# Broadcasts of norm roots as transposes, state-space products by row halves, and sample's score pairs, in one layer of a hybrid encoder

## The chip, the cores and the metric

The kernel runs on one core of one Trainium2 chip. The metric is the time of one execution on the device in microseconds (us). The core has a matrix engine (TensorE, PE in the profile, whose weight loads are listed apart as PEld), VectorE (DVE), ScalarE (ACT), GpSimd (POOL) and SyncE (SP). SyncE issues the DMAs here, in order. Each engine works through its own queue in order and waits on semaphores for the others.

## The reference

One inference step of one layer (depth 1, width 1024, float32) for 2048 prompt frames and 32 sample frames that continue a stream of 2048 earlier frames:

```python
h = x + RMSNorm(Mixer(RMSNorm(x)))
y = h + RMSNorm(ConvFFN(RMSNorm(h)))
```

The mixer makes one input projection and runs two groups of 8 heads of 64 beside each other. Group A is stick-breaking attention: with scores z, the weight of key k is sigmoid(z_k) times the product of sigmoid(-z_j) over all later keys j up to the query, strictly causal. Group B is a state-space scan (Mamba-2) in 2 groups of 4 heads with state 64, behind a causal convolution of width 4. Both outputs are RMS-normalised and projected. The ConvFFN is a gated MLP with hidden width 2816 and a causal convolution of width 3 on the gate.

Three things in it matter here. Every RMSNorm needs, for each frame, the root 1 / sqrt(mean of squares + eps). In each chunk of the scan, `cb = C B^T` and `C h` are needed for each of the two groups of heads, where h is the state. The 32 sample frames attend to 2048 cached keys of 8 heads.

## The kernel before

**Tiling.** Features lie on the partitions and frames along the free axis. The 2080 frames are cut into four blocks of 512, 512, 512 and 544 (`SBS`; the last holds the 32 sample frames). Matrix products are exact in float32 by splitting both operands into a high and a low part; `dense` (line 180) multiplies the three products that matter. The attention's products (lines 910, 951) work on such parts too. Small products are plain float32 matmuls.

**Stages.** `phase_in` goes over the four blocks: norm, projection, convolution, the state-space chunks of 128 frames (16 of the prompt and one of sample, 32 frames wide), keys and queries, gate. Then `Attention.heads(0, ...)` runs the first block's attention in 32 slots (8 heads x 4 query blocks); the last block's gate is woven into it as a filler, and every third slot takes one step of `sample`. From then on `heads(s)` for the next block is woven with `Tail.stream` of the block before (output projection, residual, norms, the gated MLP). The last block's tail runs alone (`Tail.alone`, from about 2380 us).

**Order.** The program is written in this order, but the order of each engine's queue is made by the planner of the compiler from a simulated timeline (`schedule_with_timeline_sim=True`). `pin`, `mark` and `behind` add dependencies that keep some fillers behind a given matmul.

**Norm roots** (`rstd_steps`, lines 214 to 273). Line 222 sums the squares over the partitions: each block of 128 frames gives one column of up to 128 rows. GpSimd raises to the power -1/2 (line 245) into `v`. Line 257 then spreads each column over all 128 partitions: a matmul with the column, read as 128 equal columns, as the stationary operand and the identity as the moving one:

```python
mm = nc.tensor.matmul(
    ps[:, c0 : c0 + q], v[:, b : b + 1].to_broadcast([P, P]), self.ident[:, :q], start=True, stop=True
)
```

It is called for the norm of each input block (4 or 5 columns), for the gate's norm of the last block (5), and for each half of each block in `norm_in`, `residual`, `root` and `finish` (2 columns, or 3 with a narrow one of 16 rows in the last block). The tiles are named `st`, `o` and `u` in the profile, the column `rn_v` or `rn_w`.

**State-space products** (lines 536 to 546). For each chunk, group g uses partitions 64 g to 64 g + 63: one product of line 540 (`cb`) and two of line 542 (`C h`), first all three of group 0, then all three of group 1. Each group writes a PSUM bank of its own. VectorE reads both behind them.

**Sample's scores** (`sample`, lines 794 to 831). Five pieces of keys (32 new ones, then four of 512) by two groups of four heads make ten steps. A step takes two loads `sk` of 256 KB (tile of 128 x 512, two buffers, lines 805 to 808), and each of them feeds one matmul of line 809 that fills one half of the partitions of the score tile `z`. Then follow the sigmoids, the scan (line 761), transposes (line 820) and the product with the values (line 825). The values' loads `sv` (line 800) have four buffers.

Of the kernel before, what the change touches and what calls it, by code (L numbers as in the profile page):

```python
# [8 lines left out]
F32 = mybir.dt.float32  # L9
# [23 lines left out]
P = 128  # L33
# [6 lines left out]
DH = 64  # L40
# [30 lines left out]
class Kernel:  # L71
# [139 lines left out]
    def rstd_steps(self, pool, psp, pt, sq, n, width, tag="rstd", out=None, rcol=None, of=None, stay=False, pin=False):  # L211

        nc = self.nc
        nb = (n + P - 1) // P
        nf, e = divmod(n, P)
        ps = psp.tile([P, 512], F32, name=pt)
        for b in range(nb):
            q = min(P, n - b * P)  # L220
            for i, t in enumerate(sq):
                mm = nc.tensor.matmul(  # L222
                    ps[:q, b : b + 1], t[:, b * P : b * P + q], self.ones[:, 0:1],
                    start=i == 0, stop=i == len(sq) - 1,
                )
                if pin and b + i == 0:
                    self.pin(mm)
        if pin:
            self.mark(mm)
        v = pool.tile([P, 8], F32, name="rn_v")  # L230
        if e:
            nc.vector.memset(v[:], 1.0)
        for rows, cols in ((slice(0, P), slice(0, nf)),) + (((slice(0, e), slice(nf, nb)),) if e else ()):
            if of is None:
                nc.vector.tensor_scalar(
                    v[rows, cols], ps[rows, cols], 1.0 / width, EPS, op0=ALU.mult, op1=ALU.add
                )
            else:
                nc.vector.scalar_tensor_tensor(
                    v[rows, cols], ps[rows, cols], 1.0 / width, of[rows, cols], op0=ALU.mult, op1=ALU.add  # L240
                )
        w = v
        if rcol is not None:
            w = pool.tile([P, 8], F32, name="rn_w")
        nc.gpsimd.tensor_tensor(w[:, :nb], v[:, :nb], self.mhalf[:, :nb], op=ALU.pow)
        if rcol is not None:
            nc.gpsimd.tensor_scalar(rcol[:, :nb], v[:, :nb], EPS, 0.0, op0=ALU.mult, op1=ALU.add)
        v = w
        yield
        ps = psp.tile([P, 512], F32, name=pt)  # L250
        r = ps if stay else pool.tile([P, 544], F32, name=tag) if out is None else out
        for b in range(nb):
            q = min(P, n - b * P)
            if b == 4:
                nc.scalar.copy(r[:, :512], ps[:])
            c0 = b % 4 * P
            mm = nc.tensor.matmul(
                ps[:, c0 : c0 + q], v[:, b : b + 1].to_broadcast([P, P]), self.ident[:, :q], start=True, stop=True
            )
            if pin and b == 0:  # L260
                self.pin(mm)
        if pin:
            self.mark(mm)
        if nb == 5:
            nc.scalar.copy(r[:, 512:n], ps[:, : n - 512])
        elif not stay:
            nc.scalar.copy(r[:, :n], ps[:, :n])
        self.rcol = v
        yield r


def phase_in(kn, ctx):
    nc, tc, a, o = kn.nc, kn.tc, kn.a, kn.o
# [102 lines left out]
    for s, (t0, nt) in enumerate(SBS):  # L376
# [25 lines left out]
        for c, then in zip(order, (*order[1:], None)):  # L402
# [5 lines left out]
            for c0, c1 in tiles_of(nt):  # L408
                ps = psd.tile([P, 512], F32, name="o")
# [34 lines left out]
        for b in range(nb):  # L444
            q = min(P, nt - b * P)
# [3 lines left out]
            for h in range(2):  # L449
                for k in range(KC):  # L450
                    for i, (l, rr) in enumerate(((xhi, wv[0]), (xlo, wv[0]), (xhi, wv[1]))):
                        nc.tensor.matmul(  # L452
                            vp[h][:q, :260], l[k][:, b * P : b * P + q], rr[:, k, h * 260 : h * 260 + 260],
                            start=i == 0 and k == 0, stop=i == 2 and k == KC - 1,
                        )
            v = sd.tile([P, 520], F32, name="v")
# [40 lines left out]
        ps = psm.tile([P, 512], F32, name="st")  # L497
# [10 lines left out]
        ps = psm.tile([P, 512], F32, name="st")  # L508
# [6 lines left out]
        for b in range(nb):  # L515
            q = min(P, nt - b * P)
# [18 lines left out]
            nc.scalar.activation(eA[:, :, :q], eA[:, :, :q], AF.Exp)  # L535
            h_in = hS if b == 4 else hT[state["h"]]
            cy = psy.tile([P, 2, 512], F32, name="y")
            for g in range(2):
                rows = slice(g * 64, g * 64 + 64)
                nc.tensor.matmul(cy[:q, g, :q], bc[rows, 0, sl], bc[rows, 1, sl], start=True, stop=True)  # L540
                for i in range(2):
                    nc.tensor.matmul(
                        cy[:, g, P + i * q : P + i * q + q],
                        h_in[rows, 2 * i : 2 * i + 2, :].rearrange("p h d -> p (h d)"), bc[rows, 1, sl],
                        start=True, stop=True,
                    )
# [14 lines left out]
            ps = psm.tile([P, 512], F32, name="st")  # L561
# [11 lines left out]
            ps = psm.tile([P, 512], F32, name="st")  # L573
# [41 lines left out]
        for name, dst in (("wk", kn.kS), ("wq", kn.qS)):  # L615
            for c in range(4):
# [4 lines left out]
                for c0, c1 in tiles_of(nt):  # L621
                    ps = psd.tile([P, 512], F32, name="o")
                    kn.dense(ps, w, xs, c0, c1)
                    n = c1 - c0
# [83 lines left out]
class Attention:  # L708
# [60 lines left out]
    def sample(self, ctx, pu):  # L769
# [22 lines left out]
        for kc in (4, 3, 2, 1, 0):  # L792
# [7 lines left out]
                    nc.sync.dma_start(v[i][:], a["cvv"][:, 4 * kc + i, :])  # L800
            for g in range(2):
                z = self.pz.tile([P, 512], F32, name="z")
                for i in range(2):
                    c = 2 * g + i
                    k = kp.tile([P, 512], F32, name="sk", bufs=2)
                    nc.sync.dma_start(
                        k[:, :n], kn.kF[:, c, :] if kc == 4 else a["ck"][c][:, 512 * kc : 512 * kc + 512]
                    )
                    nc.tensor.matmul(
                        z[DH * i : DH * i + DH, :n], qp[:, c, :], k[:, :n], start=True, stop=kc < 4  # L810
                    )
                if kc == 4:
                    nc.tensor.matmul(z[:, :n], kn.identb[:], mk[:], start=False, stop=True)
                w, end = self.weights_of(z[:, :n], n, prev[g], own[g])
# [855 lines left out]
```

## Time and profile before

| what | us |
|---|---|
| median of 3 runs | 2902.88 |
| lowest, highest | 2899.2, 2905.06 |
| the profiled execution | 2897.34 |
| its span, from the first to the last instruction | 2895.5 |

The profile shows that one execution. TensorE's mean granted clock in it is 0.985 of full speed. The page's first part gives, for each engine, busy time, share of the span and number of instructions. The page's chain follows the work that ended last back to the start, and gives its shares by engine. A row of a group reads: line, engine, operation, output <- inputs, rows*columns of the array that are used and shapes, count | busy us, mean ns of one | idle us of the engine just before them and what ended that. A row of the timeline reads: start, length, engine, line, operation, tiles, count, and in brackets an idle time before it. In a view by stretches each row has a stretch's length, the busy time of the five engines with their counts, the granted clock, the share of the DMA engines and GB/s. Bars of matmuls that follow each other overlap.

### The profile page before, as it was taken

The page shows a single profiled execution, that of the slowest core. Times are in us where ns is not written, and L with a number is a line of the kernel's source. Part 1 is how long each engine was busy: PE and PEld are TensorE (multiplying, and loading weights), DVE is VectorE, ACT ScalarE, POOL GpSimd, SP SyncE. Part 2 cuts the span into 40 slices and gives each one's busy share as a digit, 9 for nine tenths or more (in the row PEclk, how much of TensorE's full clock was granted, in tenths as well). Part 3 has the DMA queues.
Part 4 walks back from the last instruction along what each step waited for, and adds up shares of the span by engine and source line. Part 5 has one row for each costly group of instructions (what it writes and reads, how often), then busy time and mean ns, then how long its engine had stood idle before and what let it go on. Part 6 is the DMA issues. An engine that isn't in the chain of part 4 may idle for free.

```text
span 2895.5 us, 46167 instructions
## 1 busy us (share of the span) xinstructions
PE 2798.5 (97%) x16771; PEld 2416.4 (83%) x16771; DVE 1651.0 (57%) x2628; ACT 1217.8 (42%) x2568; POOL 1134.5 (39%) x1065
## 2 busy tenths in 40 slices
PE   7999999988999999999999999989999999999998
PEld 6878789976978888887888888978888889999997
DVE  7594747367564554557555555785666653623333
ACT  4343434246555454455433334654444443321111
POOL 3534242224566666556322223453223323511113
PEclk9999999999999999999999999999999999999999
DMA  8889695878767787875755556666555555755566
GB/s 291 269 303 304 240 305 206 244 227 263 233 232 265 273 273 253 274 257 192 227 169 182 183 179 227 207 202 196 172 168 171 167 176 184 249 178 178 170 177 204
DMA packets 348644, 642.04 MB, mean 222 GB/s; under 512 B 73498, under 2 KB 192930, under 8 KB 338690
## 3 DMA queue, kind: packets, MB, share of 16 engines
q1 hardware_dynamic: 348418, 639.09, 67.9%
q8 instruction: 134, 2.20, 0.3%
q14 instruction: 92, 0.75, 0.1%
HBM read 482.40 MB, written 156.57 MB: 221 GB/s over the span
## 4 chain that ended last, share of the span: by engine, by line
PE 77%; DVE 11%; DMA 6%; issue 3%; ACT 2%; POOL 1%; SPq 1%; DVEq 0%; ACTq 0%; POOLq 0%
PE o L180 39%; PE u L180 12%; PE t L180 11%; PE z L910 4%; PE pa L951 4%; PE pt L929 4%; DVE xc L425 2%; PE o L452 1%; DMA acB<-acD 1%; DVE prow L761 1%; DVE xlo L1099 1%; DVE f L1427 1%; DMA vS<-vs 1%; DMA o_kT<-kf 1%; PE u L222 1%
## 5 line engine op out<-in xcount | busy, mean ns | idle before, releaser
L180 PE MATMUL o<-xhi,w 128*128 128x512 f32 (+2 forms) x3968 | 1041.2, 344 | 17.9 <-ACT xhi L355 7.7
L180 PEld LDWEIGHTS o<-xhi,w 128*128 128x128 f32 x3968 | 694.4, 191 | 111.1 <-ACT xhi L355 7.7
L180 PE MATMUL o<-xlo,w 128*128 128x512 f32 (+2 forms) x1984 | 679.7, 343 | 1.5 <-DVE xlo L356 1.1
L766 POOL TENSOR_TENSOR beta<-beta,prow 128x512 f32<-128x512 f32 (+3 forms) x256 | 255.9, 1000 | 511.1 <-DVE prow L761 427.9
L180 PEld LDWEIGHTS o<-xlo,w 128*128 128x128 f32 x1984 | 377.6, 190 | 44.4 <-DVE xlo L356 1.6
L180 PE MATMUL u<-xhi,w 128*128 128x512 f32 x1056 | 351.3, 398 | 0.0
L180 PE MATMUL o<-ah,w 128*128 128x512 f32 x992 | 342.7, 402 | 3.4 <-DVE f L1395 3.3
L161 POOL TENSOR_TENSOR w<-wraw,w 128x512 fp32r<-128x512 f32 (+3 forms) x178 | 243.1, 1368 | 155.2 <-ACT w L160 127.8
L1347 POOL TENSOR_TENSOR y<-y,gb 128x512 f32<-128x512 f32 (+1 forms) x88 | 116.0, 1318 | 457.7 <-ACT gb L1346 457.4
L934 DVE TENSOR_TENSOR wt<-pt,wt 128x512 fp32r<-128x512 f32 (+2 forms) x320 | 191.6, 601 | 155.0 <-ACT wt L933 153.0
L761 DVE TENSOR_TENSOR_SCAN prow<-gam,prow,z 128x513 f32<-128x513 f32 x192 | 245.0, 1277 | 58.4 <-ACT beta L759 58.1
L933 ACT CAST wt<-pt 128x512 fp32r<-128x512 f32 (+2 forms) x320 | 167.3, 525 | 237.8 <-PE pt L929 235.9
L180 PEld LDWEIGHTS u<-xhi,w 128*128 128x128 f32 x1056 | 198.6, 188 | 46.2
L180 PEld LDWEIGHTS o<-ah,w 128*128 128x128 f32 x992 | 187.1, 189 | 45.8 <-DVE f L1395 4.4
L180 PE MATMUL u<-xlo,w 128*128 128x512 f32 x528 | 209.1, 396 | 0.0
L758 ACT ACTIVATE gam<-z 128x512 f32<-128x512 f32 (+2 forms) x320 | 173.0, 541 | 66.0 <-PE z L910 40.0
L180 PE MATMUL o<-al,w 128*128 128x512 f32 x496 | 196.7, 396 | 0.0
L180 PE MATMUL t<-xhi,w 128*128 128x272 f32 x960 | 189.4, 293 | 3.3 <-DMA w<-wS_outw 2.1
L929 PE MATMUL pt<-ident,beta 128*128 128x128 f32 x1088 | 182.8, 277 | 4.7 <-DVE wt L934 4.6
L1339 DVE SCALAR_TENSOR_TENSOR y<-gb,cv,y 128x512 f32<-128x512 f32 (+1 forms) x176 | 143.2, 813 | 69.1 <-ACT y L1337 66.0
L951 PE MATMUL pa<-wt,v 128*64 128x256 f32 (+3 forms) x1152 | 173.2, 281 | 7.7 <-DVE wt L934 5.5
L160 ACT CAST w<-wraw 128x512 fp32r<-128x512 f32 (+3 forms) x178 | 113.0, 635 | 158.5 <-PE o L180 93.1
(288 smaller groups left out, 4907.6 us busy)
## 6 DMA issues: line engine op xcount, KB each, us to landing
w<-wS_up SPq DMA_DIRECT2D x264, 512.0 KB, 3.5
w<-wS_dn SPq DMA_DIRECT2D x144, 384.0 KB, 3.5
w<-wS_outw SPq DMA_DIRECT2D x94, 512.0 KB, 6.2
wS_up<-w SPq DMA_DIRECT2D x88, 512.0 KB, 3.6
wraw<-wup SPq DMA_DIRECT2D x88, 256.0 KB, 4.2
k<-kS SPq DMA_DIRECT2D x80, 256.0 KB, 3.8
v<-vS SPq DMA_DIRECT2D x80, 256.0 KB, 3.7
w<-wS_bx SPq DMA_DIRECT2D x18, 1024.0 KB, 5.3
```

What stands on the lines that cost most here:

```text
L161: nc.gpsimd.tensor_tensor(lo, raw[:, :m, :], hi.bitcast(F32), op=ALU.subtract)
L180: mm = nc.tensor.matmul(ps[:, : c1 - c0], l, r, start=first and i == 0 and k == 0, stop=last and i == 2 and k == len(w) - 1, **({"skip_gro ...
L758: nc.scalar.activation(g[:, c0:512], z, AF.Sigmoid, scale=-0.125)
L761: nc.vector.tensor_tensor_scan(back(pr), back(g), z[:, 0:1].to_broadcast([P, n + 1]), self.kn.ones[:, 0:1] if prev is None else prev, op0= ...
L766: eng.tensor_tensor(b[:, :n], b[:, :n], pr[:, c0 + 1 : 513], op=ALU.mult)
L910: mm = nc.tensor.matmul(z[:, :n], q[:, P * b : P * b + P], k[:, :n], start=e == 0, stop=e == 1 and kc < s)
L929: mm = nc.tensor.transpose(t[:, P * j : P * j + P], w[:, P * j : P * j + P], kn.ident[:])
L933: nc.scalar.copy(hi, t)
L934: kn.exit = nc.vector.tensor_tensor(lo, t, hi.bitcast(F32), op=ALU.subtract)
L951: nc.tensor.matmul(av[:m, 2 * P * p + c0 : 2 * P * p + 2 * P], v[:, j, :m], wt[:, rest, j, c0:], start=kc == s and p + j + rest == 0, stop ...
L1339: nc.vector.scalar_tensor_tensor(y[:, :W], gb[:, i : i + W], kn.col(wc + i), y[:, :W], op0=ALU.mult, op1=ALU.add)
L1347: nc.gpsimd.tensor_tensor(y[:, :W], y[:, :W], t, op=ALU.mult)
```

## The change

```diff
             c0 = b % 4 * P
-            mm = nc.tensor.matmul(
-                ps[:, c0 : c0 + q], v[:, b : b + 1].to_broadcast([P, P]), self.ident[:, :q], start=True, stop=True
-            )
+            mm = nc.tensor.transpose(ps[:, c0 : c0 + q], v[:q, b : b + 1].to_broadcast([q, P]), self.ident[:q, :q])
...
-            for g in range(2):
-                rows = slice(g * 64, g * 64 + 64)
+            half = [slice(g * 64, g * 64 + 64) for g in range(2)]
+            for g, rows in enumerate(half):
                 nc.tensor.matmul(cy[:q, g, :q], bc[rows, 0, sl], bc[rows, 1, sl], start=True, stop=True)
-                for i in range(2):
+            for i in range(2):
+                for g, rows in enumerate(half):
                     nc.tensor.matmul(
                         cy[:, g, P + i * q : P + i * q + q],
...
             for g in range(2):
                 z = self.pz.tile([P, 512], F32, name="z")
-                for i in range(2):
-                    c = 2 * g + i
-                    k = kp.tile([P, 512], F32, name="sk", bufs=2)
-                    nc.sync.dma_start(
-                        k[:, :n], kn.kF[:, c, :] if kc == 4 else a["ck"][c][:, 512 * kc : 512 * kc + 512]
-                    )
-                    nc.tensor.matmul(
-                        z[DH * i : DH * i + DH, :n], qp[:, c, :], k[:, :n], start=True, stop=kc < 4
-                    )
+                k = kp.tile([P, 2, 512], F32, name="sk", bufs=2)
+                src = kn.kF[:, 2 * g : 2 * g + 2, :]
+                if kc < 4:
+                    src = a["ck"][2 * g : 2 * g + 2, :, 512 * kc : 512 * kc + 512].rearrange("c p n -> p c n")
+                nc.sync.dma_start(k[:, :, :n], src)
+                for c0 in range(0, n, 256):
+                    c1 = min(n, c0 + 256)
+                    for i in range(2):
+                        nc.tensor.matmul(
+                            z[DH * i : DH * i + DH, c0:c1], qp[:, 2 * g + i, :], k[:, i, c0:c1],
+                            start=True, stop=kc < 4,
+                        )
```

The first edit spreads a column by a transpose: the column's q rows, read as 128 equal columns, are transposed against the q x q identity, so that 128 partitions get q equal rows. The second one issues the products of the two groups in turn: both `cb`, then both first products with the state, then both second ones. The third one loads the keys of both halves of a score tile by one DMA of 512 KB into one tile (two buffers of 128 x 2 x 512, twice the memory), and multiplies them in pieces of 256 keys, the halves in turn.

## The prediction

> **What bounds the kernel now.** I read the page first, then the busy time by stage, then TensorE's groups by line, and last the timeline at the three places that the change touches.
>
> ```profile
> span 2895.5 us, 46167 instructions
> PE 2798.5 (97%) x16771; PEld 2416.4 (83%) x16771; DVE 1651.0 (57%) x2628; ACT 1217.8 (42%) x2568; POOL 1134.5 (39%) x1065
> ...
> PE 77%; DVE 11%; DMA 6%; issue 3%; ACT 2%; POOL 1%; SPq 1%; DVEq 0%; ACTq 0%; POOLq 0%
> ```
>
> TensorE is busy for 97% of the span, and 77% of the chain that ended last is its own work; VectorE and the DMAs hold most of the rest. So a matmul that goes is worth time in most places, but not in all. The stages say where, in this view by stretches (length, TensorE busy, weight load, VectorE, ScalarE, GpSimd, clock, DMA):
>
> ```profile
> 0.00:600.00 600.00, 569.86 (x3489) 483.14 (x3489) 382.72 (x708) 236.51 (x397) 223.63 (x165) 0.99 0.80 266
> 600.00:726.00 126.00, 109.26 (x767) 85.09 (x764) 84.72 (x141) 74.05 (x189) 49.38 (x65) 0.91 0.82 259
> 726.00:2380.00 1654.00, 1625.86 (x8724) 1362.96 (x8723) 981.41 (x1347) 790.31 (x1727) 725.07 (x701) 0.99 0.65 211
> 2380.00:2896.00 516.00, 493.54 (x3803) 485.20 (x3802) 202.19 (x434) 116.95 (x256) 136.44 (x135) 0.98 0.62 195
> ```
>
> 0 to 600 us is the input phase with the state-space chunks: 30 us idle. 600 to 726 is sample's attention woven into the first attention block: TensorE idles 16.7 of 126 us, and the granted clock is lowest, 0.91. The two stretches behind hold nearly all the norm roots and leave TensorE idle 28 and 22 us. "Busy" needs care: one matmul's bar is 0.27 us long, but the next starts 0.11 us later, so I count from start to start.
>
> **Part 1, norm roots.** The groups of line 257, and an existing transpose for comparison:
>
> ```profile
> L929 PE MATMUL pt<-ident,beta 128*128 128x128 f32 x1088 | 182.8, 277 | 4.7 <-DVE wt L934 4.6
> ...
> L257 PE MATMUL u<-ident,rn_v 128*128 128x128 f32 (+1 forms) x108 | 16.6, 282 | 6.1 <-POOL rn_v L245 6.1
> ...
> L257 PE MATMUL u<-ident,rn_w 128*128 128x128 f32 (+1 forms) x36 | 5.1, 268 | 0.0
> L257 PE MATMUL st<-ident,rn_v 128*128 128x128 f32 (+1 forms) x34 | 4.7, 278 | 0.0
> ...
> L257 PE MATMUL o<-ident,rn_v 128*128 128x128 f32 (+1 forms) x10 | 1.4, 272 | 0.0
> ```
>
> The code broadcasts 94 columns (17 in the input phase, 5 for the gate's norm, 54 + 18 for the rest), and the groups hold 108 + 36 + 34 + 10 = 188: each float32 matmul is two instructions. The attention's transposes (line 929) number 8 heads x (10 + 26 + 42 + 58) blocks = 1088, and the group holds 1088: one instruction each. So 94 go. What one is worth shows in the starts:
>
> ```profile
> 733.58 0.60 PE L929 MATMUL pt<-ident,beta 128*128 128x128 f32 x4
> 733.93 0.71 PE L951 MATMUL pa<-wt,v 128*64 128x256 f32 x4
> ...
> 742.88 0.60 PE L257 MATMUL u<-ident,rn_v 128*128 128x128 f32 x4
> 743.25 0.49 PE L180 MATMUL o<-xhi,w 128*128 128x256 f32 x2
> ```
>
> Two broadcasts (4 instructions) hold the engine from 742.88 to 743.25, 0.37 us; four transposes hold it 0.35 us. An instruction of either kind costs the same, and within a block the step is 0.111 us ((0.37 less 0.03 to the next matmul) / 3). A broadcast saves one step. Ten of the 94 are narrow (16 or 32 rows, the sample's): their second instruction is cheap already, and as transposes they read only 16 or 32 rows, a shape that the trace has for no transpose. The nearest row is the narrow sum of line 222:
>
> ```profile
> 2454.94 0.36 PE L222 MATMUL u<-ones,sqt 128*128 128x1 f32 x2
> 2455.23 0.20 PE L222 MATMUL u<-ones,sq 128*16 128x1 f32 x2
> ```
>
> The last full instruction starts at 2455.05, the first narrow one 0.18 us later instead of 0.11: a change of shape costs about 0.07 us on the way in, and I allow the same out. Bounds for a narrow one: -0.1 (no change of shape) to +0.2 us; I take +0.1. Sum: 84 x 0.111 = 9.3, less 10 x 0.1 = **8.3 us of TensorE** (bounds 7.3 to 10.3).
>
> A rule speaks against this part. The Trainium skill, "TensorE: Matmul & The Clock Gate", Part 4, says that transposes do not count as activity for the clock, so that full clock does not engage for them, and gives some 275 ns for one; the trace agrees with that as a bar (277 ns) but not as a price, since four of them take 0.35 us. By the rule part 1 would be worth nothing, by the rows 8.3 us.
>
> **Part 2, state-space products.** One of the 17 chunks, and the products of line 580, which already alternate between two column halves:
>
> ```profile
> 50.81 0.48 PE L540 MATMUL y<-bc 64*128 64x128 f32 x2
> 51.14 0.27 PE L542 MATMUL y<-bc,hT 64*128 64x128 f32 x1
> 51.15 0.37 PE L540 MATMUL y<-bc 64*128 64x128 f32 x1
> 51.25 0.27 PE L542 MATMUL y<-bc,hT 64*128 64x128 f32 x1
> 51.36 0.27 PE L540 MATMUL y<-bc 64*128 64x128 f32 x1
> 51.36 0.71 PE L542 MATMUL y<-bc,hT 64*128 64x128 f32 x6
> ...
> 131.46 1.09 PE L580 MATMUL y<-acB,xdt 128*64 128x128 f32 x16
> ```
>
> Six products are twelve instructions, from 50.81 to 52.07 (51.36 + 0.71): 1.26 us. The halves do run side by side already, but the second half's first product starts at 51.15, 0.34 us after the first half's. Alternated, it should start at once, as on line 580, where 16 instructions take 1.09 us, that is 8 steps of two; six steps of the same would take 1.09 - 2 x 0.11 = 0.87 us. Between 0.34 and 0.39 I take the late start, 0.33, rounded down: 17 x 0.33 = **5.6 us of TensorE**. Bounds: 0 (the planner puts other work into the block, or row halves don't follow the column halves) to 6.6.
>
> **Part 3, sample's scores.** The line's group, two of the pairs as they stand now, and a pair that falls together:
>
> ```profile
> L809 PE MATMUL z<-sk,qp 128*64 128x512 f32 (+1 forms) x40 | 14.9, 542 | 6.9 <-DMA sk<-ck 3.0 <-DMA sk<-kF 2.3 <-DMA k<-kS 1.3
> ...
> 634.65 1.07 PE L809 MATMUL z<-sk,qp 128*64 128x512 f32 x2 [0.71 <-DMA sk<-ck]
> ...
> 637.18 1.07 PE L809 MATMUL z<-sk,qp 128*64 128x512 f32 x2
> ...
> 653.61 1.08 PE L809 MATMUL z<-sk,qp 128*64 128x512 f32 x4
> ...
> 681.71 0.59 PE L809 MATMUL z<-sk,qp 128*64 128x512 f32 x1
> 682.14 1.04 PE L825 MATMUL u<-sv,swt 128*64 128x128 f32 x12
> ...
> 698.36 1.04 PE L809 MATMUL z<-sk,qp 128*64 128x512 f32 x2 [2.34 <-DMA sk<-ck]
> ...
> 708.21 1.07 PE L809 MATMUL z<-sk,qp 128*64 128x512 f32 x2
> ```
>
> A score half alone takes 1.07 us (two instructions); both halves together take 1.08 us. Of the eight long pairs three fall together now (653.61 is one); five lie 2 to 10 us apart, each half behind its own load. Together they save 5 x 1.0 = 5.0. Three of those halves already run beside sample's value products (681.71 goes on at 682.14, 0.43 instead of 0.59 us later; some 0.3 to 0.4 each), which I take off: 1.1. [...] Left: **3.4 us** (bounds 0 to 5.0).
>
> Then the waits. Both buffers are taken by one pair now, so a pair's loads go out only when the pair before has been multiplied; here each buffer holds a whole pair, and the load can go out a step earlier, ahead of what it feeds by more than a load's time:
>
> ```profile
> DMA to landing us min/median/max: 3.0/6.5/8.3
> ```
>
> So the 3.0 us behind `sk<-ck` should go; the 2.3 us behind the first `sk<-kF` stay, since that load has nothing to go ahead of. On SP's queue 20 issues become 10. Against it: a pair now waits for all 512 KB, and behind that wait on TensorE stand the attention's next scores and transposes; behind the load on SP's queue stand q, k and v of the next head. Bounds of the wait: -5.3 (both go) to +4 us (two steps late by 2 us each, like the one at 698.36); I take **-3.0**.
>
> **Sum.** TensorE loses 8.3 + 5.6 + 3.4 = 17.3 us. What hides part of it is the quarter of the chain that isn't TensorE's: the chunk recurrence and its loads in the input phase, the sigmoids and scans in sample's stage. I let 77% through, the chain's share: 13.3 us. With the wait, 16.3 us. The profiled execution took 2897.3 us (its span 2895.5 and 1.8 around it), so 2881.0; the median of the three runs shown is 2902.9, 5.6 us above it, so I forecast 2886.6, rounded to **2887 us**. Its own range: all 8.3 + 5.6 + 3.4 with 5.3 of waits is -22.6, TensorE's share alone with part 2 at nothing is -(8.3 + 3.4) x 0.77 = -9.0: 2880 to 2894.
>
> **Rivals.**
> *The roots gain nothing*: transposes let the granted clock fall, and one at half pace takes 2 x 0.111 = 0.22 us, what the two instructions take now. Then (5.6 + 3.4) x 0.77 + 3.0 = 9.9, 2893 us. For it: the clock is lowest where small work and gaps mix (0.91). Against: 1088 transposes stand in stretches with clock 0.98 and above. Chance 0.04. This is what the rule of Part 4 would come to.
> *The score pairs don't do what they say*: the planner sets the pieces apart again, or the load still goes out late. Part 3 gives 0: 13.9 x 0.77 = 10.7, 2892 us. For it: five of eight pairs are apart now. Against: one load releases both. Chance 0.07.
> *The cover holds*: the shortened work only waits longer for the scans, the recurrence and the loads. Only the share of it that stands in dense stretches counts, at the least 0 to 5 us: 2898 to 2903. For it: the 30 and 16.7 us of idle time in the two stages where parts 2 and 3 lie. Against: part 1, mostly in stretches 98% busy. Chance 0.13.
> *Slower: the planner moves the roots against their own wait.* All order comes from a simulated time, and a cheaper broadcast may be put right behind the GpSimd power that feeds it. The price is in the group above: 6.1 us behind `rn_v`, of which the view of waits says:
>
> ```profile
> PE u L257 <- POOL rn_v L245: 6.1, 4, 2.2
> ```
>
> Four of the 32 roots there (`u` in the groups of line 257) wait now, 1.5 us each. Eleven more would eat the 16.3 us; 18 more make 27 - 16.3 = +11, 2914 us. For it: every edit deals the order anew. Against: most roots are pinned behind attention's scores or come by steps of the stream. Chance 0.09.
>
> **How the numbers follow.** The forecast case has 0.67. About 0.2% (5.8 us) is what a measurement of this kernel can tell from no change. Faster: the forecast and the first two rivals, less a little of their upper ends: 0.76. Same: the cover, and those ends: 0.15. Slower: 0.09. The range takes in all gains with a better deal of the order (-22.6, and 8 us more, about a quarter of the 28 us that TensorE idles from 726 to 2380): 2872. Above it goes to the end of the covered case, 2903.
>
> **What would show it.** Line 257: 94 instructions instead of 188, one root of two blocks 0.37 to about 0.15 us. Lines of the state products: both halves' first instructions within 0.01 us, a chunk at 0.9 us. Score pairs: pieces of 256 side by side, no wait on `sk<-ck`, and fewer issues by 10; the stretch from the first score to the first root of the output shorter by 5 us or more, its clock above 0.91. The forecast is wrong if the waits behind `rn_v`, the scans or `w<-wS_up` grow by what TensorE lost.

## The result and the profile after

| | median us | runs |
|---|---|---|
| before | 2899.84 | 6 |
| after | 2892.56 | 6 |

The ratio is 0.9973, with a 95% interval of 0.9961 to 0.9985: the kernel became 7.8 us faster (4.3 to 11.3). The forecast was a gain of 16.3 us and a time of 2887 us. The range of 2872 to 2903 us holds the time, and the sign is right, but the gain is half of what was worked out. The profiled execution took 2892.87 us, close to its median; that of before took 2897.34 us, 2.5 us below its own. Single executions of one kernel spread over some 5 us to either side of the median, so where spans are compared below, that is their grain.

The page of after, its first parts and its chain:

```profile
span 2891.1 us, 46021 instructions
PE 2782.8 (96%) x16709; PEld 2405.6 (83%) x16709; DVE 1653.0 (57%) x2628; ACT 1217.8 (42%) x2568; POOL 1133.7 (39%) x1065
...
PE 77%; DMA 8%; DVE 8%; issue 3%; ACT 2%; POOL 1%; SPq 1%; DVEq 0%; ACTq 0%; POOLq 0%
```

TensorE's busy time fell from 2798.5 to 2782.8 us, by 15.7; the forecast counted 17.3. But its idle time, span less busy time, rose from 97.0 to 108.3 us. Eleven of the 15.7 us came back as waits, and the DMAs' share of the chain went from 6 to 8%.

The three edits did what they say. The groups of the lines, by TensorE:

```profile
L257 PE MATMUL u<-ident,rn_v 128*128 128x128 f32 (+1 forms) x54 | 10.6, 276 | 4.0 <-POOL rn_v L245 4.0
L810 PE MATMUL z<-sk,qp 128*64 128x256 f32 (+1 forms) x72 | 10.4, 403 | 5.6 <-DVE prow L760 3.6 <-DMA sk<-kF 2.0
L257 PE MATMUL u<-ident,rn_w 128*128 128x128 f32 (+1 forms) x18 | 3.4, 267 | 0.0
L257 PE MATMUL st<-ident,rn_v 128*128 128x128 f32 (+1 forms) x17 | 2.7, 273 | 0.0
L257 PE MATMUL o<-ident,rn_v 128*128 128x128 f32 (+1 forms) x5 | 0.8, 266 | 0.0
```

Line 257 holds 54 + 18 + 17 + 5 = 94 instructions instead of 188, and its waits behind `rn_v` are shorter than before (4.0 against 6.1). No wait on `sk<-ck` is left; the one on `sk<-kF` is. The timeline shows a root block of two, a state-space chunk and a score pair, each with the row behind it:

```profile
127.25 0.49 PE L538 MATMUL y<-bc 64*128 64x128 f32 x4
127.57 0.61 PE L541 MATMUL y<-bc,hT 64*128 64x128 f32 x8
128.12 0.33 PE L573 MATMUL st<-ident,bc 128*128 128x128 f32 x1
...
642.33 1.08 PE L810 MATMUL z<-sk,qp 128*64 128x256 f32 x8
643.24 0.82 PE L827 MATMUL u<-sv,swt 128*64 128x128 f32 x12
...
761.42 0.38 PE L257 MATMUL u<-ident,rn_v 128*128 128x128 f32 x2
761.55 0.37 PE L180 MATMUL o<-xhi,w 128*128 128x256 f32 x1
```

From start to start, a chunk takes 128.12 - 127.25 = 0.87 us, a pair 0.91 and a root of two blocks 0.13 (it was 0.37). The stages of the prediction's view, the last 4 us shorter:

```profile
0.00:600.00 600.00, 563.30 (x3452) 477.33 (x3453) 388.60 (x708) 236.75 (x396) 223.19 (x165) 0.98 0.81 266
600.00:726.00 126.00, 110.96 (x849) 91.18 (x848) 90.26 (x150) 79.30 (x201) 54.26 (x69) 0.92 0.84 268
726.00:2380.00 1654.00, 1621.46 (x8675) 1358.04 (x8673) 978.43 (x1346) 786.54 (x1720) 723.44 (x700) 0.99 0.64 212
2380.00:2892.00 512.00, 487.04 (x3738) 479.06 (x3738) 195.68 (x425) 115.16 (x252) 132.82 (x132) 0.97 0.59 190
```

Idle time is now 36.7 us in the input phase (30 before), 15.0 in sample's stage (16.7), 32.5 (28.1) and 25.0 (22.5) behind it. So the waits grew in the input phase and in the two dense stretches, which the forecast had not expected, and the mean granted clock fell from 0.985 to 0.982.

Two of the longer waits can be read directly. At the start of the convolution, the value weights are split by ScalarE (line 300) and VectorE (line 301). TensorE's timeline before and after at that place:

```profile
58.62 0.39 PE L452 MATMUL o<-wvhi,xhi 128*128 128x260 f32 x1 [3.90 <-ACT wvhi L302]
58.85 0.28 PE L452 MATMUL o<-wvhi,xlo 128*128 128x260 f32 x1
58.97 0.33 PE L452 MATMUL o<-wvhi,xhi 128*128 128x260 f32 x1
...
63.77 0.59 PE L452 MATMUL o<-wvlo,xhi 128*128 128x260 f32 x1 [4.26 <-DVE wvlo L303]
```

```profile
60.02 0.59 PE L450 MATMUL o<-wvhi,xhi 128*128 128x260 f32 x1 [5.80 <-ACT wvhi L300]
60.40 0.42 PE L450 MATMUL o<-wvhi,xlo 128*128 128x260 f32 x1
60.62 0.42 PE L450 MATMUL o<-wvhi,xhi 128*128 128x260 f32 x1
...
66.54 0.58 PE L450 MATMUL o<-wvlo,xhi 128*128 128x260 f32 x1 [5.29 <-DVE wvlo L301]
```

Both waits are longer, 11.1 us instead of 8.2. And the matmuls behind the longer one start 0.22 us apart (60.40 to 60.62) instead of the 0.12 us of before (58.85 to 58.97). Such a wait costs its own time, and here it costs again in the slower matmuls behind it.

### The profile page after: what moved, and what is told of

It reads as the page before. It is cut to its first block, busy times and chain, and to the rows that moved or that the text cites. A ratio compares the mean times of both kernels' runs of the same rounds, so it can differ in the third digit from the quotient of the medians.

```text
span 2891.1 us, 46021 instructions
## 1 busy us (share of the span) xinstructions
PE 2782.8 (96%) x16709; PEld 2405.6 (83%) x16709; DVE 1653.0 (57%) x2628; ACT 1217.8 (42%) x2568; POOL 1133.7 (39%) x1065
## 4 chain that ended last, share of the span: by engine, by line
PE 77%; DMA 8%; DVE 8%; issue 3%; ACT 2%; POOL 1%; SPq 1%; DVEq 0%; ACTq 0%; POOLq 0%
PE o L180 39%; PE u L180 12%; PE t L180 11%; PE z L912 4%; PE pa L953 4%; PE pt L931 3%; PE o L450 2%; DMA w<-wS_outw 1%; DVE xc L423 1%; DVE prow L760 1%; DVE f L1429 1%; DMA acB<-acD 1%; DMA eA<-acD 1%; DMA wraw<-wk 1%; DVE xlo L1101 1%
## 5 line engine op out<-in xcount | busy, mean ns | idle before, releaser
L180 PE MATMUL o<-xhi,w 128*128 128x512 f32 (+2 forms) x3968 | 1042.7, 345 | 15.7 <-ACT xhi L353 7.6
L757 ACT ACTIVATE gam<-z 128x512 f32<-128x512 f32 (+2 forms) x320 | 173.0, 541 | 58.1 <-PE z L912 32.4
```

Of the source, the lines that this page charges most:

```text
L180: mm = nc.tensor.matmul(ps[:, : c1 - c0], l, r, start=first and i == 0 and k == 0, stop=last and i == 2 and k == len(w) - 1, **({"skip_gro ...
L757: nc.scalar.activation(g[:, c0:512], z, AF.Sigmoid, scale=-0.125)
```

## The experiments

The expectations name four theories. **A**: the products and scores stood beside other waits, so that their saving only lengthened these (the cover). **B**: the forecast, an even share of what TensorE loses, and a small change of order. **C**: the compiler orders by its own estimate of times, and with the cheaper broadcasts it makes another order, which is worse at a few joints between stages. **D**: a transpose itself costs more than the forecast took. The parts are numbered as in the prediction.

Each kernel was timed beside the kernel before on the same chip.

| kernel | median us | before us | ratio (95%) |
|---|---|---|---|
| part 1 alone | 2902.95 | 2902.14 | 1.0000 (0.9990 to 1.0010) |
| part 2 alone | 2899.02 | 2902.14 | 0.9989 (0.9977 to 1.0001) |
| part 3 alone | 2889.80 | 2902.14 | 0.9957 (0.9942 to 0.9972) |
| parts 1 and 3 | 2897.06 | 2902.14 | 0.9979 (0.9970 to 0.9989) |
| parts 2 and 3 | 2887.07 | 2903.14 | 0.9944 (0.9925 to 0.9963) |
| all, other half first | 2894.51 | 2903.14 | 0.9970 (0.9956 to 0.9984) |
| all, each transpose twice | 2890.96 | 2903.14 | 0.9960 (0.9947 to 0.9973) |
| all, state products twice | 2911.99 | 2903.14 | 1.0026 (1.0011 to 1.0042) |
| 2 and 3, pairs not in pieces | 2893.47 | 2900.86 | 0.9980 (0.9968 to 0.9992) |
| 2, and four buffers for 3 | 2889.99 | 2900.86 | 0.9965 (0.9954 to 0.9976) |
| 2 and 3, roots of the input phase | 2890.43 | 2900.86 | 0.9963 (0.9950 to 0.9976) |
| 2 and 3, all the other roots | 2889.17 | 2900.86 | 0.9956 (0.9940 to 0.9973) |

### One part at a time

Part 1 alone, beside the kernel before:

```diff
-            mm = nc.tensor.matmul(
-                ps[:, c0 : c0 + q], v[:, b : b + 1].to_broadcast([P, P]), self.ident[:, :q], start=True, stop=True
-            )
+            mm = nc.tensor.transpose(ps[:, c0 : c0 + q], v[:q, b : b + 1].to_broadcast([q, P]), self.ident[:q, :q])
```

> Part 1 alone, on the kernel before. After the whole change TensorE idles 11 us more than before (span less busy time: 97.0 to 108.3 us), so what went was time that TensorE had been given back. Theory A (the input phase and the stages with waits cover the savings; only work in dense stretches passes): the roots lie mostly in dense stretches, so -4 to -8 us, ratio 0.997 to 0.9985. Theory B (every saving passes at 77%, and a new deal of the planner's order took some 8 us back): -6 us plus or minus the deal. Both expect 94 instructions on line 257 and two-column roots at 0.14 us instead of 0.36.

It gained nothing (within 2.9 us either way), where the forecast gave it 8.3 x 0.77 = 6.4 us, and both theories some 4 to 8 us.

Part 2 alone:

```diff
-                for i in range(2):
+            for i in range(2):
+                for g, rows in enumerate(half):
                     nc.tensor.matmul(
                         cy[:, g, P + i * q : P + i * q + q],
```

> Part 2 alone. A: the chunk's block takes 0.87 instead of 1.19 us, 5.4 us less TensorE work in the input phase, but the phase ends at the same time within 1.5 us, because TensorE waits there for the split of the wv weights and for the copies out of PSUM; the time is the same within 3 us (ratio 0.999 to 1.001). B: -4 us, ratio 0.9986, and the input phase ends 4 us earlier.

3.2 us by the ratio, with an interval from 6.7 us to none; forecast 5.6 x 0.77 = 4.3. That doesn't decide between A and B. Nor does the trace: the attention behind the input phase starts 2.6 us earlier (its first wait on line 910, now 911, ends at 602.90 instead of 605.46 us), which is more than A's 1.5 and less than B's 4.

Part 3 alone:

```diff
-                    k = kp.tile([P, 512], F32, name="sk", bufs=2)
+                k = kp.tile([P, 2, 512], F32, name="sk", bufs=2)
...
+                nc.sync.dma_start(k[:, :, :n], src)
+                for c0 in range(0, n, 256):
```

> Part 3 alone. A: the stretch from the first score to the first root of the output norm is shorter by 7 to 9 us, as in the changed kernel, and the time falls by 5 to 9 us (ratio 0.997 to 0.998). B: -5.6 us, ratio 0.998, give or take the deal.

12.5 us (8.1 to 16.8), twice the 5.6 us of the forecast and more than either theory gave it. Alone it is as fast as the whole change.

Parts 1 and 3, which is the whole change with part 2 taken back:

```diff
-            for i in range(2):
-                for g, rows in enumerate(half):
+                for i in range(2):
                     nc.tensor.matmul(
                         cy[:, g, P + i * q : P + i * q + q],
```

> The change without part 2. A: as fast as the whole change within 2 us (ratio about 0.997). B: 4 us slower than the whole change (ratio about 0.9985).

With part 1 beside it, part 3 is worth 6 us instead of 12.5: the ratio went from 0.9957 to 0.9979, and the two intervals overlap by a hair only. Between A (0.997) and B (0.9985) the interval decides nothing.

Parts 2 and 3, the whole change with part 1 taken back:

```diff
-            mm = nc.tensor.transpose(ps[:, c0 : c0 + q], v[:q, b : b + 1].to_broadcast([q, P]), self.ident[:q, :q])
+            mm = nc.tensor.matmul(
+                ps[:, c0 : c0 + q], v[:, b : b + 1].to_broadcast([P, P]), self.ident[:, :q], start=True, stop=True
+            )
```

> The change without part 1. Part 1 alone came out at 1.0 although its broadcasts are as much cheaper as worked out, and its trace stands still in the dense stretches and loses in steps at four joints between stages (near 50, 820, 1950 and 2520 us). Theory C: the roots' saving is real, but the order that the planner makes around them puts other waits on those joints; without part 1 the joints stay as before, and this is the fastest of all: -12 to -16 us, ratio 0.9945 to 0.996. Theory B (every part passes alike): 6 us slower than the whole change, ratio 0.9995.

0.9944: this is the fastest kernel of the study, ahead of the whole change by 0.0029, about 8 us (their intervals meet at 0.996). So the roots don't just gain nothing; in the company of the other two parts they cost about what they were to bring. The kernel with the other half first (below), which has the whole change's work and was timed in the same session as this one, gives the same: 2894.51 against 2887.07 us.

### Is it the transpose, or what it does to the order?

The whole change, with each transpose issued twice into the same place:

```diff
-            mm = nc.tensor.transpose(ps[:, c0 : c0 + q], v[:q, b : b + 1].to_broadcast([q, P]), self.ident[:q, :q])
+            for _ in range(2):
+                mm = nc.tensor.transpose(ps[:, c0 : c0 + q], v[:q, b : b + 1].to_broadcast([q, P]), self.ident[:q, :q])
```

> The whole change with each transposed broadcast issued twice: 94 more instructions, 10.4 us more TensorE work at 0.111 us each. Theory C: dense stretches lose 0.2 us for each two-column root, but the joints are dealt anew, and the time lies anywhere from 6 us faster to 10 us slower than the whole change. Theory D: 8 to 15 us slower than the whole change (ratio 1.000 to 1.0025), since each transpose brings its price again. Even passing at 77%: 8 us slower, ratio 1.000.

188 transposes, about as dear as the old broadcasts, and the kernel isn't slower than with 94 (0.9960 against 0.9973). By theory D it had to lose. Its first joint looks as before: the split of the value weights waits 3.9 + 3.9 us, not 5.8 + 5.3. The Trainium skill, "TensorE: Matmul & The Clock Gate", Part 4, says that transposes don't count as activity for the clock; here the kernel with 188 of them has a mean clock of 0.986, the same as parts 2 and 3 with none in their place, so that this run doesn't show it.

The whole change, with the second row half first:

```diff
-            for g, rows in enumerate(half):
+            for g, rows in reversed(list(enumerate(half))):
                 nc.tensor.matmul(cy[:q, g, :q], bc[rows, 0, sl], bc[rows, 1, sl], start=True, stop=True)
             for i in range(2):
-                for g, rows in enumerate(half):
+                for g, rows in reversed(list(enumerate(half))):
```

> The whole change with the two row halves in the other turn (group 1 first): the same instructions and the same work on every engine. Theory C: the planner makes another order from it, and the time moves by 2 to 6 us either way against the whole change (0.9973), in steps at the joints. Theory D (what part 1 loses is the price of a transpose itself, by the clock or by changes of shape): the same within 1.5 us, and the same losses at the same joints.

The same time as the whole change, with the same waits at the same joints (5.8 + 5.3 us at the split). By the letter this is what D expected, and C missed: it had put another order and 2 to 6 us. But the planner made no other order here. Counted in order of time, the sequences of ScalarE's and VectorE's instructions and of SyncE's transfers are those of the whole change without one exception. So this run can't tell C from D; it shows that the same order gives the same time, and that not every edit of the program deals the order anew.

The last two runs split part 1 by stage, on top of parts 2 and 3: transposes only for the input blocks' norms (17 columns, tile `st`), and only for all others (77 columns).

```diff
-            mm = nc.tensor.transpose(ps[:, c0 : c0 + q], v[:q, b : b + 1].to_broadcast([q, P]), self.ident[:q, :q])
+            if pt != "st":
+                mm = nc.tensor.matmul(
+                    ps[:, c0 : c0 + q], v[:, b : b + 1].to_broadcast([P, P]), self.ident[:, :q], start=True, stop=True
+                )
+            else:
+                mm = nc.tensor.transpose(ps[:, c0 : c0 + q], v[:q, b : b + 1].to_broadcast([q, P]), self.ident[:q, :q])
```

> Parts 2 and 3 whole, and of part 1 only the 17 columns of the four input blocks' norms as transposes; the other 77 stay matmuls. Theory C (the cheaper broadcast makes another order, with new waits at the joints): the split of the value weights at 50 to 66 us waits 11 us as in the whole change instead of 8, and that joint is the only one that is lost, so the time is 2 to 4 us over that of parts 2 and 3 together: 0.9950 to 0.9965; if the joint at 50 us keeps its old order, 0.994. Theory B (17 x 0.111 us times 77%, a gain of 1.5 us): 0.9939. Theory D (a transpose costs more than it saves, evenly): 17 of 94 of the 8 us that part 1 costs, 0.9949.

```diff
-            if pt != "st":
+            if pt == "st":
```

> Parts 2 and 3 whole, and part 1 except for the 17 columns of the input blocks' norms: 77 columns as transposes. Theory C: the joint at 50 to 66 us keeps the order of before (8 us of waits), the joints at 800 to 825 and 1935 to 1950 us and at the start of the last tail lose as in the whole change: 0.9955 to 0.9970, clock from 800 to 830 us at 0.8 or below. Theory B: 0.9924 (7 us of transposes saved times 77% below 0.9944). Theory D: 77 of 94 of the loss, 0.9968; it differs from C in that the loss is spread evenly over the stages and not in steps at joints.

Both ratios lie between those of parts 2 and 3 (0.9944) and of the whole (0.9973). Their intervals overlap with both, so the ratios alone decide nothing; the stretches of the trace do. The view by stretches, in the columns of the prediction, for three joints. Parts 2 and 3 without roots:

```profile
50.00:75.00 25.00, 15.98 (x110) 15.17 (x109) 16.54 (x23) 10.14 (x16) 13.01 (x8) 0.80 0.53 165
800.00:830.00 30.00, 28.91 (x153) 24.65 (x154) 21.37 (x29) 15.38 (x35) 20.65 (x19) 0.93 0.52 169
2495.00:2530.00 35.00, 32.35 (x254) 31.72 (x253) 17.83 (x35) 8.64 (x20) 11.62 (x10) 1.00 0.79 258
```

The whole change:

```profile
50.00:75.00 25.00, 13.33 (x87) 12.43 (x86) 18.19 (x22) 9.87 (x15) 13.38 (x8) 0.73 0.58 197
800.00:830.00 30.00, 25.92 (x116) 20.09 (x117) 25.26 (x38) 16.87 (x43) 16.19 (x17) 0.77 0.51 167
2495.00:2530.00 35.00, 30.59 (x225) 30.18 (x225) 19.60 (x38) 8.30 (x18) 10.83 (x10) 0.90 0.73 243
```

Roots of the input phase alone:

```profile
50.00:75.00 25.00, 13.25 (x84) 12.30 (x83) 18.52 (x22) 9.87 (x15) 12.84 (x8) 0.73 0.58 192
800.00:830.00 30.00, 30.00 (x157) 25.34 (x156) 20.22 (x26) 14.29 (x31) 19.57 (x18) 0.95 0.57 190
2495.00:2530.00 35.00, 33.12 (x259) 32.39 (x259) 19.92 (x41) 9.82 (x21) 12.03 (x12) 1.00 0.84 266
```

All the other roots:

```profile
50.00:75.00 25.00, 16.51 (x119) 15.60 (x119) 16.58 (x23) 10.14 (x16) 13.99 (x9) 0.80 0.58 185
800.00:830.00 30.00, 25.87 (x126) 20.45 (x126) 23.04 (x33) 16.11 (x40) 17.36 (x16) 0.86 0.44 142
2495.00:2530.00 35.00, 29.73 (x224) 29.32 (x222) 18.89 (x39) 8.96 (x19) 12.10 (x11) 0.95 0.74 241
```

Read TensorE's busy time and instructions, and the clock. With cheap roots in the input phase the first joint falls to 13.3 us of work in 25 (84 to 87 instructions, clock 0.73); without, it does 16.0 to 16.5 (clock 0.80). The second and the third go by the other roots: 25.9 against 28.9 to 30.0 us, and 29.7 to 30.6 against 32.4 to 33.1. Each set of roots switches the joints of its own stage and no others. The clock from 800 to 830 us is 0.86 with the other roots, not 0.8 or below as put. The joint at 1935 to 1950 us falls as put: TensorE works 11.5 of 15 us with the other roots, 15.0 in parts 2 and 3.

That it is the order shows when the traces' sequences of instructions are laid beside each other. For each engine's queue I counted how many instructions stand out of the sequence of parts 2 and 3 (matched by line and tile in order, line 257 itself left out), of ScalarE's 2568 instructions and of some 3245 records of SyncE's queue:

| kernel, beside parts 2 and 3 | ScalarE before 600 us | ScalarE after | SyncE before 600 us | SyncE after |
|---|---|---|---|---|
| roots of the input phase | 43 | 0 | 203 | 0 |
| all the other roots | 0 | 283 | 0 | 467 |
| the whole change | 43 | 282 | 203 | 467 |
| the whole, each transpose twice | 0 | 119 | 0 | 43 |

The whole change's order is the two halves' put together, and with the broadcasts made dear again most of the old order is back, although every broadcast is still a transpose. This decides for C against D.

The new order isn't worse everywhere. Against parts 2 and 3, TensorE's same instructions (matched in order, median of a stretch of some 30 to 120 us) start later by

| kernel, beside parts 2 and 3 | from 726 us | from 1000 us | from 1400 us | from 1980 us | span |
|---|---|---|---|---|---|
| all the other roots | 1.2 | 6.3 | 1.3 | 7.5 | 6.3 |
| the whole change | 5.5 | 10.1 | 1.0 | 4.0 | 6.6 |

Some 5 us are lost near 800 us, 5 to 9 us come back near 1250 us, and 3 to 6 are lost again near 1900 us. In single executions such a difference is good to some 3 us: that much lies between the whole change and the kernel with the other half first, whose order is the same. The run with the input phase's roots starts the same instructions 2.5 us later from 75 us and 0.8 us earlier from 640 us, and from 600 us its order is that of parts 2 and 3. So the loss at its joint was made up in this execution, and where the time behind its ratio of 0.9963 went isn't shown.

What the order costs at one joint can be followed at 2498 us, in SyncE's timeline (start, length, line, transfer). Parts 2 and 3:

```profile
2498.36 0.38 SPq L152 DMA_DIRECT2D w<-wS_up  x1
2498.83 0.38 SPq L1436 DMA_DIRECT2D o_yT<-f  x1
2499.31 0.38 SPq L152 DMA_DIRECT2D w<-wS_up  x1
2499.78 1.27 SPq L1436 DMA_DIRECT2D o_yT<-f  x2
2501.14 0.41 SPq L152 DMA_DIRECT2D w<-wS_up  x1
2501.99 2.93 SPq L1436 DMA_DIRECT2D o_yT<-f  x5
2505.02 1.22 SPq L152 DMA_DIRECT2D w<-wS_up  x2
```

The whole change:

```profile
2498.50 1.34 SPq L152 DMA_DIRECT2D w<-wS_up  x3
2499.97 6.28 SPq L1434 DMA_DIRECT2D o_yT<-f  x7
2506.29 0.44 SPq L1335 DMA_DIRECT2D o_fconv<-gb  x1
2506.79 0.44 SPq L1336 DMA_DIRECT2D o_fconv<-gb  x1
2507.33 0.86 SPq L152 DMA_DIRECT2D w<-wS_up  x2
```

and TensorE behind it:

```profile
2511.06 0.57 PE L180 MATMUL t<-xhi,w 128*128 128x272 f32 x1 [4.30 <-DMA w<-wS_up]
```

Seven output stores in a row hold the queue for 6.28 us, the next two weight loads go out at 2507.33 instead of 2505.02, and TensorE waits 4.30 us for the first of them. Where the stores stand between the loads, in parts 2 and 3, the only wait on `w<-wS_up` in this stretch is 0.62 us:

```profile
2502.41 0.39 PE L180 MATMUL t<-xhi,w 128*128 128x272 f32 x1 [0.62 <-DMA w<-wS_up]
```

The run with all the other roots has the seven stores in a row too (6.21 us from 2502.45), and there TensorE waits 1.63 us for a load and 3.64 us behind VectorE.

### Does the input phase have cover to spare?

The whole change, with all six products of a chunk issued twice:

```diff
+            for _ in range(2):
+                for g, rows in enumerate(half):
+                    nc.tensor.matmul(cy[:q, g, :q], bc[rows, 0, sl], bc[rows, 1, sl], start=True, stop=True)
+                for i in range(2):
+                    for g, rows in enumerate(half):
...
```

> The whole change with the six state-space products of each chunk issued twice: 17 x 0.66 = 11 us more TensorE work, all in the input phase. If the waits of the input phase cover TensorE there: the phase ends less than 4 us later, ratio below 0.999. If TensorE sets the pace there: the phase ends 8 to 11 us later, ratio 1.000 to 1.001.

0.0053 above the whole change, 15 us, above the 1.000 to 1.001 of the case in which TensorE sets the pace. A chunk takes 1.54 us from start to next in its trace instead of 0.87, which is 17 x 0.67 = 11.4 us of added work, and the input phase ends 9 to 11 us later (in an execution that lies 7 us below its median). It has a new order of its own too: 38 of ScalarE's instructions before 600 us stand out of the whole change's sequence, and one of its roots waits 4.09 us behind `rn_v` at 149 us. So the two aren't cleanly apart here; but the added work was not swallowed, as theory A would have it, so the cover is unlikely to be what took the gain.

### What part 3 is made of

Parts 2 and 3, but one load for a pair and whole products of 512 keys:

```diff
-                for c0 in range(0, n, 256):
-                    c1 = min(n, c0 + 256)
-                    for i in range(2):
-                        nc.tensor.matmul(
-                            z[DH * i : DH * i + DH, c0:c1], qp[:, 2 * g + i, :], k[:, i, c0:c1],
+                for i in range(2):
+                    nc.tensor.matmul(
+                        z[DH * i : DH * i + DH, :n], qp[:, 2 * g + i, :], k[:, i, :n], start=True, stop=kc < 4,
```

> Parts 2 and 3 without the roots (0.9944 with all of part 3), but the score products are not cut into pieces: one load for a pair, then the two products of 512 keys, one half behind the other. This splits part 3. Load theory (the pair's load goes out a step earlier and releases both halves at once; two halves that stand together run beside each other in any case, as the pair at 653.61 us of the kernel before did in 1.08 us): 0.9935 to 0.9960, sample's stage still some 8 us shorter, no wait on sk<-ck, a pair at about 1.08 us instead of 0.91. Alternation theory (the halves must be issued in turn in pieces to share the array): each half takes its 1.07 us, eight pairs lose some 1 us each, 0.9970 to 0.9990. Theory C adds some 0.001 of another order to either.

Part 2, and of part 3 only the memory:

```diff
-                    k = kp.tile([P, 512], F32, name="sk", bufs=2)
+                    k = kp.tile([P, 512], F32, name="sk", bufs=4)
```

> Parts 2 and 3 without the roots, but part 3 is only the memory that it takes: two loads of 256 KB and two products as before, with four buffers sk instead of two, so that a pair's loads can go out a step earlier. If the wait behind the loads was the larger part (5.3 us behind sk<-ck and sk<-kF before, and what stands behind them): 0.9940 to 0.9965, the wait on sk<-ck gone. If one release for both halves and their falling together are the larger part: five of eight pairs stay apart, and the time is near that of part 2 alone, 0.9975 to 0.9990.

By its ratio the first kernel (0.9980) lies in the range of the alternation theory, and the second (0.9965) at the upper end of the wait's. The traces decide more. Both expectations had a mistake in common: that two halves from two loads, or not cut into pieces, might stay apart or take longer. Two long pairs of the kernel with four buffers:

```profile
637.82 1.08 PE L810 MATMUL z<-sk,qp 128*64 128x512 f32 x4
638.73 0.82 PE L826 MATMUL u<-sv,swt 128*64 128x128 f32 x12
...
654.65 1.08 PE L810 MATMUL z<-sk,qp 128*64 128x512 f32 x4
655.66 0.33 PE L930 MATMUL pt<-ident,beta 128*128 128x128 f32 x1
```

All eight long pairs fall together there, and seven of them take 0.91 to 1.01 us from start to start, as in pieces (0.909 us three times here, 0.914 three times in parts 2 and 3); the wait on `sk<-ck` is gone in both kernels. How much later or earlier than in the kernel before the same instructions start, as the median over 25 us, from 600 to 725 us of the kernel before: part 2 alone goes from -2.6 to -2.0, four buffers from -3.9 to -9.0, one load without pieces from -5.0 to -10.8, all of part 3 from -3.4 to -12.7. So of the 9.3 us that sample's stage gains in these executions, some half comes from the memory alone, which lets a pair's loads go out a step earlier. By the ratio the four buffers are worth 7.0 us on top of part 2, and one load without pieces 2.6: it loses 4 us again at the joint of 800 us and 3 more up to 1350 us. Some 3 us of the stage's difference fall at 680 us, where without pieces one pair and its neighbours run at half pace (the pair takes 1.76 us from start to start, in pieces 0.89). That isn't the pieces' doing alone: with four buffers one pair takes 1.76 us as well, and the whole change, in pieces, has one of 1.91 us at 696.74. Theory C's joints are in these numbers as well: 119 of ScalarE's instructions stand out of the sequence of parts 2 and 3 in the kernel without pieces, 10 in that with four buffers. So the ratio of 0.9980 says nothing clean on the pieces; whether these gain by themselves stays open. The kernel with four buffers has nearly the order of parts 2 and 3 and lies 6 us behind it (0.9965 against 0.9944); their intervals overlap.

## Why the prediction was right, and where it failed

**The path.** That TensorE is the bound, and that less work there is time, held: parts 2 and 3 together gained 16 us (10.7 to 21.8 by the interval), and doubled products cost 15. How much of a saving comes through in the input phase isn't settled (part 2 below).

**Part 1, size right, worth wrong.** A broadcast of 128 rows takes one step of 0.112 us instead of two, the root of two blocks 0.13 instead of 0.37 us, and a narrow one costs about 0.1 us more, as assumed (a root of two and a narrow one went from 0.585 to 0.466 us, so 0.12 saved where two wide ones alone save 0.225). The 8.3 us were there. But with part 1 alone TensorE's busy time fell by only 2.7 (2798.5 to 2795.8), at a granted clock of 0.982 against 0.985, and its idle time rose by 10.7 us. These two executions lie 8 us apart (2897.34 and 2905.28 us) where the ratio is 1.0000, so a part of both figures is the spread of single executions. The net by the ratio is nothing. On top of parts 2 and 3 the busy time fell by 1.1 (2783.9 to 2782.8), the idle time rose by 7.7 (100.6 to 108.3), the clock fell from 0.986 to 0.982, and the net is a loss of 8 us; these two executions lie within 1 us of their medians.

**Part 2, right in size, its worth not resolved.** 0.325 us a chunk (1.193 to 0.869 from start to next) against 0.33; the two halves' first products start 0.007 us apart; 3.2 and 3.8 us by the two ratios (alone, and on top of part 3) against 4.3, neither clear of noise by itself. The orders of ScalarE, VectorE and SyncE are the same with it and without, so no joint of theory C is in these numbers.

**Part 3, mechanism right, size too small.** The pairs fall together and `sk<-ck` is gone, `sk<-kF` stays, all as put. It was worth 12.5 us instead of 5.6. TensorE's busy time fell by 5.3 us with part 3 alone (to 2793.2) where the forecast had 3.4, which is 5.0 less 1.1 for overlap and about 0.5 for the cutting into pieces. No run shows a price of the cutting: 0.914 us for a pair in pieces, 0.909 whole. Which of the waits and overlaps makes up the rest wasn't taken apart. The run with four buffers has the pairs together and the wait gone, the two effects that the forecast summed to 5.6, and it is worth 5 us in the stage and 7.0 by the ratio: that much was sized right. What the single load in pieces brings beyond it, some 5 to 6 us, had no term, and its cause is open.

**The step that failed** is "I let 77% through, the chain's share". It spread one share over all parts, as if time that leaves TensorE went into a fixed quarter of cover, and the sum has no term for the order that an edit makes; "every edit deals the order anew" stands only with a rival. What the runs show is no share: parts 2 and 3 together brought 16 us, where their terms taken whole come to 5.6 + 3.4 + 3.0 = 12.0, and part 1 came through with less than nothing, because its effect on the order is larger than its work. Two errors of opposite sign, 6.9 us too little for part 3 and about 14 too much for part 1 (a gain of 6.4 forecast, a loss of 8 on top of the others), left the total within 9 us. That the time fell into the range is in part luck.

**The rivals.** The one that came nearest is the last, that the planner moves the roots, given 0.09. It had the right mechanism and the wrong place: it looked for the price behind `rn_v`, where waits fell from 6.1 to 4.0 us, and not at the joints, where VectorE, ScalarE and SyncE work in the order of the same plan. The forecast did name `w<-wS_up` as a sign of its failure: on the tile `t` that wait went from 1.2 to 4.3 us, on `o` from 2.6 to 0.8. "The roots gain nothing" (2893 us) met the time of 2892.56 for a reason that isn't its own: the transposes start 0.112 us apart, at no half pace, and twice as many of them weren't slower. The covered case, which left at most 5 us of gain, falls with the 12.5 us of part 3.

**What stays open.** The planner's estimate isn't visible here: that it prices a transpose below the pair of passes is inferred from the orders, and why its order is the worse one on the chip wasn't followed beyond the two joints shown; near 1250 us it is the better one. Nor is it shown that another order with cheap roots couldn't keep the 8.3 us.

## What to carry to other kernels

In a kernel whose queues are ordered by a compiler's own timeline, an edit has two effects: the work that it takes away, and the order that the new estimate makes. Time each part alone and each left out before keeping all of them; here two parts of three were 8 us better than three. To tell the two effects apart, issue the cheap instruction twice, and lay the queues' sequences beside each other: if the time doesn't rise and the old order comes back, the order is what changed it.

## What the runs showed of the hardware

- A wait of TensorE can cost more than its length: behind a 5.80 us gap the matmuls of the value weights started 0.22 us apart, behind a gap of 3.90 us in the kernel before 0.12. The length alone doesn't decide: with all the other roots they started 0.22 us apart behind a gap of 3.90 us at the same place (58.53 us).
- Two 64-column halves of the array run side by side whether or not the program issues them in turn and in pieces: 0.91 us for a pair of 512-key products in four instructions (with four buffers at 637.82 us, the two halves start 0.007 us apart), and 0.91 us for eight pieces. What kept them apart was the second half's load.
- The halves by rows do so as well, once issued in turn: 0.87 us for twelve products of a chunk, where group after group took 1.19 us.
